# Second expert table's weights split by pairs of neighbouring indices, the first norm applied on turned rows, tiles placed anew (decoder step, one core)

## The chip, the core and the metric

The kernel runs on one core of a Trainium2 chip. TensorE (PE, its weight loads shown as PEld) multiplies, VectorE (DVE), ScalarE (ACT) and GpSimd (POOL) do the elementwise work, SyncE (SP) issues most DMAs, and POOL issues the gathers. The metric is the device time of one execution in microseconds (us); lower is better.

## The reference

One decoder layer for 256 prompt tokens and 32 sample tokens (8 sequences of 4): an input projection feeds 16 RWKV-7 heads and 16 sparse-attention heads, an output projection and a residual norm follow. Then comes the part that the change is about, a mixer over 16384 experts chosen by product keys:

```python
def peer_ffn(x, wq, subkeys, u_tab, v_tab):
    q = (xt @ wq).reshape(n, P_HEADS, 2, P_DKEY // 2)          # 8 heads, two halves of 128
    s = jnp.einsum('nhcd,hckd->nhck', q, subkeys)              # 128 keys for each half
    hv, hix = lax.top_k(s, P_TOPK)                             # 16 of each
    cand = hv[:, :, 0, :, None] + hv[:, :, 1, None, :]
    cand_e = hix[:, :, 0, :, None] * N_KEYS + hix[:, :, 1, None, :]
    tv, tpos = lax.top_k(cand, P_TOPK)                         # 16 experts for each head
    gate = jax.nn.softmax(tv, axis=-1)
    h = gelu(einsum('cd,chkd->chk', xb, u_tab[eb]))            # 128 dots for each token
    return einsum('chk,chkd->cd', gb * h, v_tab[eb])           # 128 weighted rows

x = layer_norm(DEEPNORM_ALPHA * x + h, ln1_g, ln1_b)
f = peer_ffn(x, peer_wq, peer_subkeys, peer_u, peer_v)
x = layer_norm(DEEPNORM_ALPHA * x + f, ln2_g, ln2_b)
```

All data is float32, D_MODEL is 2048. The tables peer_u and peer_v hold 16384 rows of 2048.

## The kernel before

Products are split where accuracy is wanted at a high rate: an operand is cast to float32r (the high part, on ACT), the rest is the operand less that cast (the low part, on DVE or POOL), and three matmuls high-high, high-low, low-high take the place of one in float32. The order on each engine is not the program's: a planner plays the program through on a model of the engines and issues what is ready by priority. `tc.issue_after(x)` puts instructions no earlier than x, `tc.high_priority(offset=n)` lifts them, `keep_in_program_order` pins them. Tiles live in pools that are stacks from the left and from the right of each partition; a tile placed over older ones waits until those are done with. In a pool, the first call for a name sets its place.

The stages from the output projection on, which the change touches:

1. *Output projection* (`out_part`, L1647 to L1676). `out_part(0, BV)` multiplies the RWKV half beside the prompt attention, `out_part(8, YN)` the attention half: 16 pieces of weight, each cast (L1662), split (L1663; every fourth on POOL) and used by 12 matmuls (L1668); sums go into X1 on DVE (L1674, L1676).
2. *Sample chain* (`sample_chain`, L1465 on): the 32 sample tokens go through their own projection, norm, queries and choice (`choose`, `settle`), and then through 32 rounds of two gathers of half rows of peer_u (POOL, `gather`, L454) and two dots on DVE (L1552). It is woven with `out_part(8, YN)`.
3. *First norm of the prompt tokens* (`layer_norm`, L1622): statistics (L1628), root (L1434 to L1438 and L242 to L247), normalising on ACT (L1633), gain and bias on DVE and POOL (L1634, L1635), store to X1D in memory (L1723), turning by PE (L1727), copies to XT (L1731), and casts and splits of six of its 16 blocks to XH, XL (L1639, L1640 in `columns`).
4. *Queries* (from L1745): SKT and QP are placed, X1a is read back from X1D; 16 columns of queries in float32 (L1808, ring `wraw` of four tiles), QP copies (L1809), scores (L1375) into a ring in TB of two heads, and for each head and 128 tokens `choose` on DVE with one large product on POOL (L1410) and `settle` (L1416, L1417). Heads 3 to 8 carry one dot of the gathered part each (L1777).
5. *Dense part of the first table* (`dense`, L1837): for each first key one tile `ur` of nine 128-column blocks (576 KB), three blocks in float32 (L1843), six split (L1850). The other seven blocks of 2048 columns are gathered for each chosen expert (`peer_u_g`, 128 by 896) and dotted on DVE (L1777), 1.5 for each key.
6. *Weighing* (from L1927): 64 groups of four tokens pick their activations out of AW (`pick`, `picked`, `product_of`), apply gelu and gate, and put the weights back (`scaled` on ACT, L1918; `put`, L1924); the first 28 groups carry the rest of the dots, the others the second table's rows of the samples (L1942). Then `norm_quarters` finishes the samples (L1980 to L1991).
7. *Second table* (from L1995): 128 blocks k, each 128 rows by 1408 columns of peer_v (`rows_load`, 704 KB, three buffers), cast (L2034) and split (L2035). For two blocks at once the token weights out of AW, which lies as [128, 2, 256 tokens, 64], are cast (L2031) and split (L2032). 18 matmuls (L2042) take the weights as the stationary operand. The last 640 columns are gathered for each token and expert (`rq`) and added on DVE (L2015). In the middle, x1 and the gain and bias of the last norm are loaded into the part of AW that is done with (L2056, L2060). `fin` adds, norms and stores.

Of the kernel before, what the change touches and what calls it, by code (L numbers as in the profile page):

```python
# [10 lines left out]
F32 = mybir.dt.float32  # L11
# [23 lines left out]
NSO = 4  # L35
PRI = 200
# [114 lines left out]
def hybrid_decode_step(ctx: ExitStack, tc: tile.TileContext, a, outs, dbg=None):  # L151
# [1234 lines left out]
    def choose(t, h, pool, S, TV):  # L1386
# [5 lines left out]
        gp.tensor_copy(HF, HI)  # L1392
        gp.tensor_scalar(HF[:, 0], HF[:, 0], 128.0, None, op0=OP.mult)
# [19 lines left out]
    def settle(t, h, pool, hit):  # L1413

        EF = pool([P, 16], "EF")
        ve.tensor_reduce(EF, hit, AX.X, OP.add)  # L1416
        ve.tensor_scalar(GI[t][:, 16 * h:16 * h + 16], EF, 2.0 if t == 2 else 1.0, None, op0=OP.mult)  # L1417

# [46 lines left out]
    def sample_chain(cx):  # L1465
# [76 lines left out]
        hd = cx([P, 2, 32], "hd")  # L1542
# [5 lines left out]
        for s_ in range(32):  # L1548
# [4 lines left out]
            yield 1  # L1553
        ve.tensor_tensor(hd[:, 0], hd[:, 0], hd[:, 1], OP.add)
# [49 lines left out]
    more_banks(sa=2, pb=1, sao=1, pa=2)  # L1604
    np_ = Pool("np", "left")
# [4 lines left out]
    cx = [Pool("cx", "left")]  # L1610
    lp, oe = Pool("lp", "left"), Pool("oe", "left")
# [10 lines left out]
    def layer_norm(pool, x, g_, b_):  # L1622

        st = pool([P, 4, 6], "lnst", bufs=2)
        mv = pool([P, 2], "lnmv", bufs=2)
        rr = pool([P, 1], "lnrr", bufs=2)
        for q in range(4):
            ve.bn_stats(out=st[:, q, :], in_=x(512 * q, 512))  # L1628
        ve.bn_aggr(out=mv, in_=st.rearrange("p a b -> p (a b)"))
        norm_row(pool, mv, rr)  # L1630
        for q in range(4):
            x_ = x(512 * q, 512)
            sc.activation(x_, x_, AF.Identity, bias=mv[:, 0:1], scale=rr)  # L1633
            ve.tensor_tensor(x_, x_, g_(512 * q, 512), OP.mult)  # L1634
            (gp if q % 2 else ve).tensor_tensor(x_, x_, b_(512 * q, 512), OP.add)  # L1635
# [11 lines left out]
    def out_part(o, src):  # L1647
# [7 lines left out]
        for cq in range(4):  # L1655
# [15 lines left out]
            for t in range(2):  # L1671
# [30 lines left out]
    weave((take(chain, 38), 38), (prompt_attention(), 19), (out_first(), 19))  # L1702
    M_("out")
    fewer_banks(1)
    more_banks(pa=6)
    weave((chain, 32), (out_part(8, YN), 16))
# [4 lines left out]
    XH, XL = (xq([P, NSP, NPR], nm, F32R) for nm in ("XHq", "XLq"))  # L1711
# [7 lines left out]
    for t in range(2):  # L1719
        layer_norm(lp, lambda c0, n: x1c(t, c0, n),  # L1720
                   *(lambda c0, n, nm=nm: gb1[nm, c0 // 1024][:, c0 % 1024:c0 % 1024 + n] for nm in ("ln1_g", "ln1_b")))
        for hf in range(2):
            sy.dma_start(X1D[P * t:P * t + P, 1024 * hf:1024 * hf + 1024], X1[t][hf])  # L1723
        for q in range(4):
            pb = bank("pa")
            for e in range(4):
                pe.transpose(pb[:, 128 * e:128 * e + 128], x1c(t, 512 * q + 128 * e, 128), ident)  # L1727
            tk = slice(P * t, P * t + P)
            p4, e0 = pb.rearrange("p (k t) -> p k t", k=4), max(0, 16 - NDB - 4 * q)
            e1 = min(4, 16 - NDB + NSP - 4 * q)  # L1730
            sc.copy(XT[:, 4 * q:4 * q + 4, tk], p4)  # L1731
            if e1 > e0:
                k4 = slice(4 * q + e0 - 16 + NDB, 4 * q + e1 - 16 + NDB)
                columns(p4[:, e0:e1], XH[:, k4, tk], XL[:, k4, tk])
    oe.close()
    lp.close()
    cx[0].close()
    np_.close()
# [388 lines left out]
```

## Time and profile before

| | |
|---|---|
| three runs | 2503.61, 2513.51, 2522.33 us; median 2513.51 us |
| profiled execution | 2521.09 us; its span 2518.9 us, mean granted PE clock 0.929 |
| busy | PE 2248.0, PEld 1884.6, DVE 1876.1, ACT 962.4, POOL 1374.3 us |
| memory | 683.17 MB moved by DMA, 271 GB/s on average |
| second half of the output projection | 1002.9 to 1061.1 us |
| query products | 1103.4 to about 1238 us |
| dense part | first copy to AW at about 1243 us, last at 1711.8 us |
| second table's matmuls | 1982.1 to about 2496 us |

The page cuts the span into 40 slices of 63 us and gives for each engine the busy share in tenths. A group row gives line, engine, operation, output and input, shape and count, then busy time and the mean ns of one, then the idle time of the engine just before and what ended it. A timeline row gives start, duration, engine, line, operation and, in brackets, the idle time before it and its releaser. A window row gives the busy time of PE, PEld, DVE, ACT and POOL in a stretch, with counts, then the granted PE clock, the DMA share and GB/s. A wait row gives who waited for whom: us in all, times, longest. A line row gives the shortest, median and longest duration in ns, and the first and last start.

### The profile page before, as it was taken

How to read it: one execution, taken by the hardware profiler on the slowest of the kernel's cores; microseconds unless marked ns; L12 is line 12 of the kernel's file. 1: busy time of each engine (PE TensorE's matmuls, PEld its weight loads, DVE VectorE, ACT ScalarE, POOL GpSimd, SP SyncE). 2: the span in 40 equal slices, each digit the busy share in tenths (PEclk: the TensorE clock that was granted, in tenths of full speed). 3: DMA queues.
4: the chain of work that ended last, by engine and by line, in shares of the span. 5: the costliest groups of instructions: out<-in, count | busy, mean ns of one | idle time of the engine just before them, and what ended most of it. 6: DMA issues, size and time to landing. Idle time of an engine off the chain costs nothing.

```text
span 2518.9 us, 44857 instructions
## 1 busy us (share of the span) xinstructions
PE 2248.0 (89%) x16396; PEld 1884.6 (75%) x16396; DVE 1876.1 (74%) x4266; ACT 962.4 (38%) x1847; POOL 1374.3 (55%) x1393
## 2 busy tenths in 40 slices
PE   7988999997888997749999999997689799989996
PEld 7877898874645665538888889996666688868885
DVE  5789756554553356977977777669986699989998
ACT  4433222213332343221133334444566554435453
POOL 5677423242355003754655555555556488868883
PEclk9999999997895897969999999997899899989998
DMA  8777975457468884985489999997678699999995
GB/s 225 223 234 227 270 219 168 118 177 228 168 233 252 282 278 170 344 293 182 134 340 371 370 372 351 357 353 227 205 241 291 219 364 359 361 367 353 359 365 198
DMA packets 327420, 683.17 MB, mean 271 GB/s; under 512 B 82206, under 2 KB 200928, under 8 KB 326400
## 3 DMA queue, kind: packets, MB, share of 16 engines
q1 hardware_dynamic: 246560, 343.63, 41.1%
q0 software_dynamic: 80640, 336.68, 38.2%
q8 instruction: 129, 2.11, 0.3%
q14 instruction: 91, 0.75, 0.1%
HBM read 664.64 MB, written 23.88 MB: 273 GB/s over the span
## 4 chain that ended last, share of the span: by engine, by line
PE 50%; DVE 17%; DMA 9%; POOL 9%; issue 8%; ACT 3%; SPq 1%; POOLq 0%; DVEq 0%; ACTq 0%
PE ph L1850 10%; PE pb L2042 10%; POOL rq L454 6%; PE pj L423 5%; PE ph L1843 3%; PE p L1080 2%; PE pa L1668 2%; DVE rows L1777 2%; PE pa L1924 2%; DVE ul L1640 2%; DMA co<-in_cache_cmp_kv,gidx 2%; PE pj L1808 1%; DVE cw L1552 1%; PE px L1894 1%; PE sa L921 1%
## 5 line engine op out<-in xcount | busy, mean ns | idle before, releaser
L454 POOL DMA_INDIRECT rq<-in_peer_v_g,gi x256 | 404.3, 1579 | 118.0 <-DVE fP L2015 67.8
L454 POOL DMA_INDIRECT rows<-in_peer_u_g,gi x256 | 327.0, 1277 | 249.5 <-DVE rows L1777 206.8
L1777 DVE SCALAR_TENSOR_TENSOR rows<-rows,x1a 128x896 f32<-128x896 f32 x256 | 274.3, 1100 | 2.0 <-DMA rows<-in_peer_u_g,gi 1.9
L423 PE MATMUL pj<-XH,wl 128*128 128x288 f32 (+1 forms) x752 | 231.8, 309 | 13.9 <-DVE wl L418 7.7
L423 PE MATMUL pj<-XH,wh 128*128 128x288 f32 (+1 forms) x752 | 229.7, 306 | 14.0 <-DVE ss L753 6.1
L1850 PE MATMUL ph<-XHd,uh 128*128 128x256 f32 x768 | 236.4, 308 | 0.0
L1850 PE MATMUL ph<-XHd,ul 128*128 128x256 f32 x768 | 224.6, 293 | 8.4 <-DVE ul L1640 3.6
L1640 DVE TENSOR_TENSOR ul<-ur,uh 128x384 fp32r<-128x384 f32 x256 | 133.6, 560 | 128.1 <-ACT uh L1639 88.1
L423 PE MATMUL pj<-XL,wh 128*128 128x288 f32 (+1 forms) x752 | 225.9, 301 | 0.0
L2015 DVE SCALAR_TENSOR_TENSOR fP<-rq,ge,fP 128x640 f32<-128x640 f32 x254 | 223.7, 881 | 2.4
L1850 PE MATMUL ph<-XLd,uh 128*128 128x256 f32 x768 | 217.0, 283 | 0.0
L2042 PE MATMUL pb<-vl,ah 128*128 128x512 f32 (+1 forms) x768 | 206.9, 378 | 0.0
L2042 PE MATMUL pb<-vh,ah 128*128 128x512 f32 (+1 forms) x768 | 187.7, 380 | 20.8 <-ACT vh L2034 20.8
L2042 PE MATMUL pb<-vh,al 128*128 128x512 f32 (+1 forms) x768 | 205.8, 376 | 0.0
L416 ACT CAST wh<-wraw 128x512 fp32r<-128x512 f32 (+1 forms) x188 | 115.0, 616 | 227.0 <-PE pj L423 188.3
L1843 PE MATMUL ph<-Xfd,ur 128*128 128x256 f32 x768 | 187.3, 379 | 2.4 <-DMA ur<-in_peer_u_t 2.4
L2042 PEld LDWEIGHTS pb<-vh,ah 128*128 128x128 f32 x768 | 142.9, 191 | 44.5 <-ACT vh L2034 21.9
L477 DVE SCALAR_TENSOR_TENSOR CA<-co,wbc,CA 128x256 f32<-128x256 f32 x248 | 135.6, 585 | 48.5 <-DMA co<-in_cache_cmp_kv,gidx 48.5
L1850 PEld LDWEIGHTS ph<-XHd,ul 128*128 128x128 f32 x768 | 146.5, 191 | 22.7 <-DVE ul L1640 22.0
L423 PEld LDWEIGHTS pj<-XH,wl 128*128 128x128 f32 (+1 forms) x752 | 143.9, 191 | 25.7 <-DVE wl L418 11.6
L1852 ACT COPY AW<-ph 128x256 f32<-128x256 f32 x128 | 77.8, 608 | 217.4 <-PE ph L1850 204.8
L423 PEld LDWEIGHTS pj<-XH,wh 128*128 128x128 f32 (+1 forms) x752 | 144.2, 192 | 20.7 <-ACT wh L416 6.7
(854 smaller groups left out, 5519.4 us busy)
## 6 DMA issues: line engine op xcount, KB each, us to landing
ur<-in_peer_u_t SPq DMA_DIRECT2D x128, 576.0 KB
wraw<-in_w_in SPq DMA_DIRECT2D x152, 256.0 KB
cw<-in_w_out SPq DMA_DIRECT2D x32, 512.0 KB
wraw<-in_peer_wq SPq DMA_DIRECT2D x32, 512.0 KB
wraw<-in_w_out SPq DMA_DIRECT2D x32, 512.0 KB
cw<-in_peer_wq SPq DMA_DIRECT2D x32, 512.0 KB
wraw<-in_w_in SPq DMA_DIRECT2D x64, 128.0 KB
co<-in_state_win_kv SPq DMA_DIRECT2D x16, 512.0 KB
```

The source lines that it names most:

```text
L416: sc.copy(wh[:, :, :n], w[:, :, :n])
L423: last[2] = pe.matmul(pb[:n, :nt], wi[:, k, :n], xi[(o + k) // 8][:, (o + k) % 8, :nt], start=(o + k == 0 and wi is wh and xi is xh), stop ...
L454: gp.indirect_dma_start(out=dst, out_offset=None, in_=rows_, in_offset=bass.IndirectOffsetOnAxis(ap=ix, axis=0))
L477: ve.scalar_tensor_tensor(d_, x_, w_, d_, op0=OP.mult, op1=OP.add)
L1080: pe.matmul(pb[hs[c], 64 * m:64 * m + 64], lhs(hs[c], m), rhs(hs[c], m), start=True, stop=True)
L1640: return ve.tensor_tensor(xl, pb, xh.bitcast(F32), OP.subtract)
L1777: i_ = ve.scalar_tensor_tensor(r_, r_, 1.0, X1a[t][:, :UG], op0=OP.mult, op1=OP.mult, accum_out=h_)
L1843: pe.matmul(ph[:, :NPR], w[:, e, :], Xfd[:, e - NSP, :], start=(e == NSP), stop=False)
L1850: mm = pe.matmul(ph[:, :NPR], wi[:, e - e0, :], xi[:, e, :], start=False, stop=(e == NSP - 1 and wi is wl))
L1852: return lo_, mm, sc.copy(AW[:, i1 // 64, :, i1 % 64], ph[:, :NPR])
L2015: ve.scalar_tensor_tensor(fP[t], r_, w_, fP[t], op0=OP.mult, op1=OP.add)
L2042: pe.matmul(acc[3 * t + q][:, :n_], wi[:, P * t:P * t + P], xi[:, 512 * q:512 * q + n_], start=(k == 0 and wi is ah and xi is vh), stop=(k ...
```

## The change

- *Second table.* The weights of two blocks are cast and split as [128, tokens, 2] instead of [128, 2, tokens]: AW is read by pairs of words, and TensorE reads its stationary operand at every second word.
- *Late loads of the second table's stage.* Each of the eight loads is placed after the row load of its block.
- *First norm.* Statistics are taken as each column quarter is summed; both roots are taken at once; DVE normalises; PE turns the rows without gain and bias, and ACT applies these while it copies to XT, where they are per-partition numbers. The token rows get gain (DVE) and bias (POOL) afterwards, and POOL stores them to X1D. The casts and splits for the dense part come out of XT, on ACT and POOL, at the end of the queries.
- *Sample dots.* 14 of 32 rounds stay beside the output projection, which is lifted in priority by 400; six are placed after the norm, the others at two for each head in the queries, out of a pool and a copy of the sample rows of their own. The prompt dots there start at head 7, not 3.
- *`choose`, `settle`.* The index casts go to POOL.
- *Weighing.* The last four groups share their scaling between ACT and DVE. The sample norm's loads move to group 46 and into X1a's place.
- *Tiles.* Pools are opened in another order, and names called early, so that tiles lie elsewhere: the first query weights and the first `ur`, `oT`, `v_` and `vh` tiles among them.

The diff, cut to its core:

```diff
@@ choose, settle
-        gp.tensor_copy(HF, HI)
-        gp.tensor_scalar(HF[:, 0], HF[:, 0], 128.0, None, op0=OP.mult)
+        for c in range(2):
+            gp.tensor_scalar(HF[:, c], HI[:, c], k_ if c else k_ * P, 0.0, op0=OP.mult, op1=OP.add)
-        ve.tensor_scalar(GI[t][:, 16 * h:16 * h + 16], EF, 2.0 if t == 2 else 1.0, None, op0=OP.mult)
+        gp.tensor_copy(GI[t][:, 16 * h:16 * h + 16], EF)
@@ sample_chain
-        for s_ in range(32):
+        yield from sample_dots(ring, x4, 0, NSD)                      # NSD = 14
@@ W4
+    lp = Pool("lp", "left")
+    cx = [Pool("cx", "left")]
+    oe = Pool("oe", "left")
     np_ = Pool("np", "left")
-    cx = [Pool("cx", "left")]
-    lp, oe = Pool("lp", "left"), Pool("oe", "left")
@@ out_part
                     ve.tensor_tensor(x_, x_, acc[t], OP.add)
+                    ve.bn_stats(out=lst[:, t, cq, :], in_=x_)
@@ out, ln1
-    weave((chain, 32), (out_part(8, YN), 16))
+    weave((chain, NSD), (out_part(8, YN), 16, 400))
+    wq_ = {(0, o): query_load(0, o) for o in (0, 8)}
     for t in range(2):
-        layer_norm(lp, ...)
-        for hf in range(2):
-            sy.dma_start(X1D[P * t:P * t + P, 1024 * hf:1024 * hf + 1024], X1[t][hf])
+        ve.bn_aggr(out=lmv[:, t, :], in_=lst[:, t].rearrange("p a b -> p (a b)"))
+    ...
+    for t in range(2):
         for q in range(4):
+            normed = ve.tensor_scalar(x_, x_, lrr[:, t:t + 1], lv[:, t:t + 1], op0=OP.mult, op1=OP.add)
             pb = bank("pa")
             for e in range(4):
                 pe.transpose(pb[:, 128 * e:128 * e + 128], x1c(t, 512 * q + 128 * e, 128), ident)
-            sc.copy(XT[:, 4 * q:4 * q + 4, tk], p4)
-            if e1 > e0:
-                columns(p4[:, e0:e1], XH[:, k4, tk], XL[:, k4, tk])
+            for e in range(4):
+                k = 4 * q + e
+                sc.activation(XT[:, k, P * t:P * t + P], pb[:, 128 * e:128 * e + 128], AF.Identity,
+                              bias=prm("ln1_b", 16, k), scale=prm("ln1_g", 16, k))
+    late = sample_dots(lambda: sq_([P, 1024], "sr", bufs=5), sx4, NSD, 32)
+    with tc.issue_after(normed.ins):
+        for _ in take(late, NLD):                                     # NLD = 6
+            pass
+        ...                  # X1 times ln1_g on DVE, plus ln1_b on POOL
+                gp.dma_start(X1D[P * t:P * t + P, 1024 * hf:1024 * hf + 1024], X1[t][hf])
@@ wq
-    TB = up([P, 4, NPR], "TB")
-    X1a = [up([P, UG], f"x1a{t}") for t in range(2)]
-    ...
-    kc, dp, kq = (Pool(nm, "left") for nm in ("kc", "dp", "kq"))
+    up([P, 1024], "rows", bufs=NRW)
+    xa_ = up([P, 2 * UG], "x1a")
+    TB = up([P, 4, NPR], "TB")
+    dp, kc, kq = (Pool(nm, "left") for nm in ("dp", "kc", "kq"))
+    dp([P, NDB, P], "ur", bufs=NUR)
+        if h == 2:
+            for t in range(2):
+                sy.dma_start(X1a[t], X1D[P * t:P * t + P, :UG])
             with tc.issue_after(chosen.ins):
+                for _ in take(late, 2):
+                    pass
-                if h > 2:
+                if h > 6:
                     dot(NDW, 16 * (h - 1), ahead=2)
-    sc.copy(XHd, XH)
-    sc.copy(XLd, XL)
+    for q in range(NSP // 2):
+        k2, x_ = slice(2 * q, 2 * q + 2), XT[:, 16 - NDB + 2 * q:18 - NDB + 2 * q, :]
+        sc.copy(XHd[:, k2, :], x_)
+        gp.tensor_tensor(XLd[:, k2, :], x_, XHd[:, k2, :].bitcast(F32), OP.subtract)
@@ weigh
+            if u < 60 or e % 2:
+                pin(sc.activation(o_, o_, AF.Copy, scale=g_))
+            else:
+                pin(ve.tensor_scalar(o_, o_, g_, None, op0=OP.mult))
+        if s_ == 46:
+            ...              # loads of the sample norm, into xa_ (before: after the loop, into "rows")
@@ V
     vp = Pool("vp", "left")
+    vp([P, FD], "v_", bufs=2)
+    vp([P, FD], "vh", F32R, bufs=2)
-            a2 = [vp([P, 2, NPR], nm, F32R, bufs=2) for nm in ("ah", "al")]
-            aw_ = AW[:, k // 64, :, k % 64:k % 64 + 2].rearrange("p t e -> p e t")
+            a2 = [vp([P, NPR, 2], nm, F32R, bufs=2) for nm in ("ah", "al")]
+            aw_ = AW[:, k // 64, :, k % 64:k % 64 + 2]
-        ah, al = (t_[:, k % 2, :] for t_ in a2)
+        ah, al = (t_[:, :, k % 2] for t_ in a2)
         if k + 3 < P:
-            rows_load(k + 3)
+            ld_ = rows_load(k + 3)
         if 66 <= k < 114 and k % 6 == 0:
+            with tc.issue_after(ld_.ins):
                 ...          # one of the eight late loads
```

More of the change, by code (lines that the diff above doesn't have):

```diff
@@ L1547, in sample_chain, with sample_dots @@
         ve.tensor_scalar(IG, GI[2], 1.0, None, op0=OP.add)
-        for s_ in range(32):
+        yield from sample_dots(ring, x4, 0, NSD)
+    def sample_dots(ring, x4, n0, n1):
+        for s_ in range(n0, n1):
             for q in range(2):
@@ L1609, in hybrid_decode_step @@
         np_(shape, nm, bufs=n_)
-    cx = [Pool("cx", "left")]
-    lp, oe = Pool("lp", "left"), Pool("oe", "left")
     X1 = [[lp([P, 1024], f"x1_{t}{h}") for h in range(2)] for t in range(2)]
+    lst, lmv, lrr, lv = lp([P, 2, 4, 6], "lnst"), lp([P, 2, 2], "lnmv"), lp([P, 2], "lnrr"), lp([P, 2], "lnv")
     def x1c(t, c0, n):
         return X1[t][c0 // 1024][:, c0 % 1024:c0 % 1024 + n]
[L1622 to L1635, printed above, removed]
     def columns(pb, xh, xl):
@@ L1710, in hybrid_decode_step, with query_load @@
     XT = xq([P, 16, NPR], "XT")
[L1711 removed]
+    kw_ = Pool("kw", "right")
+    wring = lambda: kw_([P, 8, P], "wraw", bufs=WB)
+    def query_load(c, o):
+        w = wring()
+        sy.dma_start(w, w_q[:, 128 * c:128 * c + 128].rearrange("(k p) c -> p k c", p=P)[:, o:o + 8])
+        return w
+    wq_ = {(0, o): query_load(0, o) for o in (0, 8)}
     M_("ln1")
@@ L1823, in hybrid_decode_step @@
         settle(t, 7, kc, hit)
+    with tc.issue_after(chosen.ins), tc.issue_after(last_.ins):
+        for _ in late:
+            pass
+        sample_formed()
+    sq_.close()
     kw_.close()
-    sc.copy(XHd, XH)
-    sc.copy(XLd, XL)
+    for q in range(NSP // 2):
+        k2, x_ = slice(2 * q, 2 * q + 2), XT[:, 16 - NDB + 2 * q:18 - NDB + 2 * q, :]
+        sc.copy(XHd[:, k2, :], x_)
+        gp.tensor_tensor(XLd[:, k2, :], x_, XHd[:, k2, :].bitcast(F32), OP.subtract)
     sc.copy(Xfd, XT[:, 16 - NDB + NSP:, :])
@@ L1972, in hybrid_decode_step @@
             smp_add(s_ - 30)
+        if s_ == 46:
+            bs_, gs_, x_ = (xa_[:, 512 * n:512 * n + 512] for n in range(3))
+            for q in range(4):
+                r_, c_ = slice(32 * q, 32 * q + 32), slice(512 * q, 512 * q + 512)
+                sy.dma_start(x_[r_, :], X1D[NPR:NT, c_])
+                for t_, nm in ((gs_, "ln2_g"), (bs_, "ln2_b")):
+                    sy.dma_start(t_[r_, :], bass.AP(tensor=a[nm].tensor, offset=a[nm].offset + 512 * q, ap=[[0, 32], [1, 512]]))
         if s_ == 50:
```

79 lines of the change are left out of this document (42 added, 37 removed).

## The prediction

> **What bounds the kernel now.** I read the page first, then the kernel stretch by stretch. The slices show one hole in PE's row, and the chain by engine says that PE alone carries half of the span.
>
> ```profile
> span 2518.9 us, 44857 instructions
> PE   7988999997888997749999999997689799989996
> PE 50%; DVE 17%; DMA 9%; POOL 9%; issue 8%; ACT 3%; SPq 1%; POOLq 0%; DVEq 0%; ACTq 0%
> ```
>
> The hole (slices of 63 us, the 18th and 19th) lies between the output projection and the query products. PE's timeline and the waits of that stretch (us in all, times, longest) explain it:
>
> ```profile
> 1002.87 0.78 PE L1668 MATMUL pa<-wh,YH 128*128 128x512 f32 x1
> 1060.64 0.39 PE L1668 MATMUL pa<-wh,YL 128*128 128x512 f32 x1
> 1060.87 0.39 PE L1668 MATMUL pa<-wl,YH 128*128 128x512 f32 x1
> PE pa L1727 <- DVE x L1635: 32.6, 4, 13.0
> 1103.43 15.61 PE L1808 MATMUL pj<-XT,wraw 128*128 128x256 f32 x64
> 1131.60 10.04 PE L1808 MATMUL pj<-XT,wraw 128*128 128x256 f32 x32 [12.56 <-ACT QP L1809]
> 1142.36 13.98 PE L1808 MATMUL pj<-XT,wraw 128*128 128x256 f32 x64
> 1156.18 1.05 PE L1375 MATMUL pb<-SKT,QP 128*128 128x128 f32 x8
> 1157.07 13.98 PE L1808 MATMUL pj<-XT,wraw 128*128 128x256 f32 x64
> 1237.51 1.34 PE L1375 MATMUL pb<-SKT,QP 128*128 128x128 f32 x8
> ```
>
> Read it so. The projection ends at 1061; the norm's turnings then wait 33 us for gain and bias on DVE; two query columns run; PE stands another 12.6 us because QP's place is free only after the last sample dot. From 1142 PE runs without a gap: 14.7 us for a head (1142.36 to 1157.07). DVE beside it:
>
> ```profile
> L1552 DVE SCALAR_TENSOR_TENSOR cw<-cw,x 128x1024 f32<-128x1024 f32 x26 | 38.8, 1512 | 1.4 <-DMA cw<-in_peer_u,gi 1.2 <-DMA cw<-in_peer_u,ig 0.2
> L1552 DVE SCALAR_TENSOR_TENSOR cw<-cw,x 128x1024 f32<-128x1024 f32 x32 | 39.8, 1249 | 11.0 <-DMA cw<-in_peer_u,gi 7.7 <-DMA cw<-in_peer_u,ig 3.2
> 1200.00:1220.00 20.00, 20.00 (x102) 17.81 (x101) 19.72 (x85) 2.60 (x7) 12.82 (x19) 1.00 0.62 170
> L1417 DVE TENSOR_SCALAR gi<-EF 128x16 int32<-128x16 f32 x12 | 12.4, 1036 | 0.2
> L1777 DVE SCALAR_TENSOR_TENSOR rows<-rows,x1a 128x896 f32<-128x896 f32 x6 | 10.1, 1680 | 0.0
> ```
>
> The first two rows are the sample dots of 1003 to 1061 and of 1061 to 1131; the others belong to the query heads. There PE is full and DVE is full too (19.72 of 20), so work moved in does not come free.
>
> The last table's stage is paced by PE, with two stalls. In its timeline the matmuls of one row block start every 3.83 us:
>
> ```profile
> 1982.05 2.71 PE L2042 MATMUL pb<-vh,ah 128*128 128x512 f32 x6 [3.66 <-ACT vh L2034]
> 1987.40 0.37 SPq L1950 DMA_DIRECT2D v__20880<-in_peer_v  x1
> 1992.60 1.36 ACT L2034 CAST vh<-v__20880 128x1408 fp32r<-128x1408 f32 x1 [9.56 <-DMA v__20880<-in_peer_v]
> 1999.57 1.44 PE L2042 MATMUL pb<-vh,ah 128*128 128x512 f32 x6
> 2191.08 1.44 PE L2042 MATMUL pb<-vh,ah 128*128 128x512 f32 x6
> 2194.91 1.44 PE L2042 MATMUL pb<-vh,ah 128*128 128x512 f32 x6
> 2224.23 2.64 SPq L2056 DMA_DIRECT2D AW<-x1d  x4
> 2233.65 1.45 PE L2042 MATMUL pb<-vh,ah 128*128 128x512 f32 x6
> 2255.21 1.44 PE L2042 MATMUL pb<-vh,ah 128*128 128x512 f32 x6
> 2242.00:2250.00 8.00, 0.65 (x2) 0.56 (x3) 0.67 (x1) 1.36 (x1) 0.00 (x0) 0.50 1.02 408
> 2300.00:2360.00 60.00, 60.00 (x284) 51.68 (x283) 58.42 (x55) 29.85 (x24) 49.01 (x32) 1.00 0.98 363
> ```
>
> Two blocks should take 7.7 us. At the start they take 17.5 (1982.05 to 1999.57), because rows 1 and 2 are asked for at 1987.40 only. In the middle they take 21.6 (2233.65 to 2255.21): all eight late loads, 4.2 MB, go out together at 2224 and the row loads queue behind them. Otherwise PE has no gap (60.00 of 60) while DVE (58.4) and DMA (0.98) stand just beneath.
>
> **The change, part by part.** Sums are made against the profiled execution, 2521.1 us: the span and 2.2 around it.
>
> *Projection, norm and sample dots.* 192 matmuls at 0.23 (1060.64 to 1060.87) are 44 us, and they took 58. With 14 of the 32 samples in this stretch and the projection raised in priority, I take 47 (bounds 44 and 58): end at 1050, not 1061. The first of the turnings' waits, 13.0 us, runs from there to the first turning; statistics are now taken as columns finish and the gain, the bias and most dots leave it, so I take 6, an estimate between 3 and 13. After them the gain and bias sit in the ACT copies behind the turnings: 32 copies at the 0.32 us of the four in the row below, so 10 us, of which the first query product needs 5 eighths. Start near 1063; 3 us for dots that get between: 1066.
>
> ```profile
> 1969.12 1.28 ACT L1918 ACTIVATE oo<-oo,TB 128x128 f32<-128x128 f32 x4
> ```
>
> Before, the gapless start that would give the same end is 1238.4 less 16 columns at 6.91 and 8 scores at 0.89 (117.7 us), so 1121. The gain here is 55 us. The waits taken away are the 33 and 12.6 above. Gain and bias on the token rows still happen, beside the query products; their stores to X1D go from SP's queue to POOL's. X1a is read back at head 2 on SP, and behind it on that queue stand the later query weights: if a store is late, they are late. The ring of four weight tiles is two columns, 14 us, of cover, so I book nothing.
>
> *What DVE pays.* Heads 1 to 6 take four sample dots each, 4 x 1.25 = 5.0 us; the integer casts leave (12.4 over 8 heads, 1.5), and in four heads a dot (1.7). Heads 3 to 6 carry 1.8 more each on a full DVE. Heads 1 and 2 had no dot to lose, but part of the 9.2 us idle in the row below, and I count 1.8 for them as well: 11 us.
>
> ```profile
> DVE HV L1363 <- ACT TB L1383: 9.2, 3, 5.3
> L1640 DVE TENSOR_TENSOR ul<-ur,uh 128x384 fp32r<-128x384 f32 x256 | 133.6, 560 | 128.1 <-ACT uh L1639 88.1
> ```
>
> Twelve more dots and eight multiplications (20 us) precede the first choice; they fit into the 21 us until the third column ends. Scores rest in a ring of two heads, so lag beyond that reaches PE. Bounds: 0 if the dense stage hides it, where DVE waits 88 us for ACT (second row); 30 if DVE paces everything and only what leaves DVE counts (12.4 + 6.7 of dots + some 6 of norm and splits = 25 of the 55). I take 12, nearer to the count above: gain 43. POOL's queue, with casts, adds and four X1D stores, has gathers behind each; its 12.8 of 20 would cover them.
>
> *Dense start.* XHd, XLd and Xfd come from XT through ACT, idle for most of the query stretch, and POOL; the first table tiles have their place early. I take 0; with the cover gone, three casts and splits at the 616 and 684 ns of the rows under *Pairs* are 4.
>
> *Weighing.* Four dots fewer in the query heads are done here, where DVE is full: the row has 1.09 each, 4.4 lost. The sample norm's loads come some fifteen groups earlier, so the 2.2 us that DVE waited for them goes, and the last four groups split their scaling: two of four 0.32 copies leave ACT, 0.64 x 4 = 2.6. Together 2.2 + 2.6 - 4.4 = +0.4.
>
> ```profile
> L1777 DVE SCALAR_TENSOR_TENSOR rows<-rows,x1a 128x896 f32<-128x896 f32 x49 | 51.4, 1086 | 0.0
> 1963.89 0.69 DVE L1987 SCALAR_TENSOR_TENSOR rows<-rows,fs 128x512 f32<-128x512 f32 x1 [2.20 <-DMA rows<-in_ln_b]
> ```
>
> *Table rows at the start.* Their buffers now lie where the sample rows lay. Those are read for the last time by the products that L1987 (1963.89, above) takes up, so both row blocks can land before 1980. The 9.8 us stall goes; what is late next is POOL's gathers, off PE's path. I take 9, bounds 0 and 10.
>
> *The burst.* One 512 KB load for six blocks: 1.376 + 0.087 MB in 3.83 us asks 382 GB/s; the rows show 363 steadily and 408 in the burst. At 371 it would cost 48 x 0.11 = 5; at 408 nothing. Of 13.9 I take 11, bounds 3 and 14.
>
> *Pairs.* The cast and the split of one table's weights read words 256 bytes apart now:
>
> ```profile
> L2031 ACT CAST ah<-AW x64: 1055/1145/1162, 1979.7 to 2480.5; 128x512 fp32r<-128x512 f32 x64
> L2032 DVE TENSOR_TENSOR al<-AW,ah x64: 1012/1109/1126, 1981.1 to 2481.7; 128x512 fp32r<-128x512 f32 x64
> L416 ACT CAST wh<-wraw 128x512 fp32r<-128x512 f32 (+1 forms) x188 | 115.0, 616 | 227.0 <-PE pj L423 188.3
> L1653 DVE TENSOR_TENSOR YL<-QT,YH 128x512 fp32r<-128x512 f32 x2 | 1.3, 684 | 0.0
> L2042 PEld LDWEIGHTS pb<-vh,ah x768: 187/188/338, 1982.1 to 2493.3; 128*128 128x128 f32 x192
> 1294.29 2.16 PE ph L1850 x18
> ```
>
> At the price of adjacent words they fall from 1145 and 1109 to some 616 and 684 ns, 0.21 us a block off DVE. PE paces, so I book 0; if DVE did, it would be 0.21 x 128 = 27, which PE's row without gaps excludes. PE now loads weights at every second word. A matmul comes every 213 ns (3.83 / 18), and the dense stage gets a load and a matmul into 120 ns (2.16 / 18), so there is room for a load of up to 1.8 times. No row shows a strided load; cost 0 at the one end, and with 376 ns unhidden (188 doubled, as the far-strided cast nearly is) 18 x 0.163 x 128 = +376 us at the other. I take 0, by the room. [...]
>
> Sum: 43 + 0.4 + 9 + 11 = 63; 2521.1 - 63 = 2458. The shown median, 2513.5, is 0.3% under the profiled run: **2450**.
>
> **Rivals.**
> *DVE and POOL pace the heads.* For it: DVE at 19.72 of 20, and instructions stretched beside POOL, L1417's 16 elements to 1036 ns, dots to 1512 and 1680 against 1086. Against: DVE idles 11 us in 1061 to 1131, and dense has room. Only 25 us come, and 5 each from the stalls: 25 + 0.4 + 5 + 5 = 35, 2478. [...]
> *All absorbed.* No lag, both stalls whole: 55 + 0.4 + 10 + 14 = 79, 2434.
> *Slower: strided weight loads.* The price is above: 2450 + 376 = 2826 unhidden. It decides once the pitch passes 240 ns (63 us over 2304 matmuls are 27 ns). At twice dense's 120 it is just there: 2450 + 60 = 2510, no change.
> *It doesn't do it.* Query products still wait for a tile that the late dots or X1D's stores hold. Then only the last stage's 20 remain: 2493.
>
> **Chances.** Forecast 0.42 (own range 2440 to 2462), DVE and POOL 0.20, all absorbed 0.20, loads unhidden 0.06, loads just hidden 0.04, not done 0.08. Faster by over 1% (25 us, about what a measurement of this kernel can tell) are the first three: 0.82; within 1%: 0.12; slower: 0.06. The range, 2415 to 2490, leaves out the loads and most of the undone case.
>
> **What will show it.** Right: query products starting near 1066 without a gap, scores about every 15 us; no PE wait on QP; blocks of 3.83 us from the first, none of 15 near block 66; al near 0.69 us and LDWEIGHTS at 188. Wrong: a pitch above 213, score distances of 17 or more, PE waiting for TB's ring, or gathers that hold POOL up at a full sample ring.

## The result, and the profile after

The changed kernel takes 2497.05 us (median of 17 runs, 2486.80 to 2508.24), the kernel before 2513.84 us in the same session (17 runs, 2501.21 to 2535.25). The ratio is 0.9932 with a 95% interval of 0.9913 to 0.9952: about 17 us, 0.7%, faster. Forecast were 2450 us and a range of 2415 to 2490: the direction is right, the size is not, and the time lies above the range. The profiled execution spans 2496.9 us. Its head, its slices of PE and its chain by engine:

```profile
span 2496.9 us, 44823 instructions
PE   7979999988889997789699999996699799999996
PE 60%; DVE 17%; DMA 8%; issue 7%; ACT 4%; POOL 3%; SPq 1%; DVEq 0%; POOLq 0%; ACTq 0%
```

The slice with a 4 is gone (the 18th has an 8 now), a 6 has come in the 20th (1186 to 1248), and PE carries 60% of the chain instead of 50%. PE's timeline around these slices:

```profile
1049.88 0.39 PE L1668 MATMUL pa<-wl,YH 128*128 128x512 f32 x1
1056.00 5.43 PE L1741 MATMUL pa<-CT,x 128*128 128x128 f32 x32 [5.74 <-DVE x L1738]
1063.27 17.53 PE L1832 MATMUL pj<-XT,wraw 128*128 128x256 f32 x80 [1.83 <-ACT XT L1744]
1100.88 1.22 PE L1378 MATMUL pb<-SKT,QP 128*128 128x128 f32 x4 [4.07 <-ACT QP L1833]
1188.84 1.34 PE L1378 MATMUL pb<-SKT,QP 128*128 128x128 f32 x8
1221.40 0.58 PE L1886 MATMUL ph<-XHd,ul 128*128 128x256 f32 x1 [21.74 <-DVE ul L1640]
```

From the projection's end to the first query product there are 13.4 us now, and the last scores are at 1189 instead of 1238. But behind them is a wait that was not there: PE reaches the dense stage and stands 21.7 us for one split of a table tile on DVE. DVE's timeline, window, group and one row of ACT say why:

```profile
1188.01 0.86 DVE L1366 MAX8 HV<-TB 128x8 f32<-128x128 f32 x4
1199.24 2.78 DVE L1559 SCALAR_TENSOR_TENSOR sr<-sr,sx 128x1024 f32<-128x1024 f32 x1
1201.96 1.22 DVE L1559 SCALAR_TENSOR_TENSOR sr<-sr,sx 128x1024 f32<-128x1024 f32 x1
1205.39 0.86 DVE L1366 MAX8 HV<-TB 128x8 f32<-128x128 f32 x4
...
1100.00:1190.00 90.00, 87.33 (x420) 77.17 (x421) 90.00 (x368) 10.82 (x29) 70.19 (x110) 0.98 0.83 257
...
L1759 DVE TENSOR_TENSOR x<-x,wraw 128x512 f32<-128x512 f32 x8 | 13.2, 1722 | 0.0
...
1097.63 0.65 ACT L1386 COPY TB<-pb 128x256 f32<-128x256 f32 x2 [12.10 <-DMA x1d<-x]
```

One head takes DVE 17.4 us (1188.01 to 1205.39) and PE 14.7; DVE is busy for 90.00 of 90 us. The split that PE waits for stands in DVE's order behind the choices of all eight heads, of which six carry four dots each. Choices also begin late: the first scores are out at 1085 and are copied at 1097.6, when the last store of the token rows has landed, over whose place TB lies.

The last stage, on SP's and PE's timelines, then the weights' rows:

```profile
1954.71 6.01 SPq L2031 DMA_DIRECT2D out<-x1a  x16
1961.09 0.37 SPq L1990 DMA_DIRECT2D v__20899<-in_peer_v  x1
1961.62 0.36 SPq L1990 DMA_DIRECT2D v__20901<-in_peer_v  x1
...
1955.08 2.71 PE L2085 MATMUL pb<-vh,ah 128*128 128x512 f32 x6 [4.22 <-ACT vh L2077]
1972.89 1.44 PE L2085 MATMUL pb<-vh,ah 128*128 128x512 f32 x6
...
2256.74 1.44 PE L2085 MATMUL pb<-vh,ah 128*128 128x512 f32 x6
2262.11 1.56 PE L2085 MATMUL pb<-vh,ah 128*128 128x512 f32 x6 [1.37 <-ACT vh L2077]
2266.44 1.44 PE L2085 MATMUL pb<-vh,ah 128*128 128x512 f32 x6
...
L2075 DVE TENSOR_TENSOR al<-AW,ah x64: 682/692/694, 1954.6 to 2459.3; 128x512 fp32r<-128x512 f32 x64
L2085 PEld LDWEIGHTS pb<-vh,ah x768: 193/193/336, 1955.1 to 2471.4; 128*128 128x128 f32 x192
```

The start is no better: two blocks take 17.8 us, as rows 1 and 2 are asked for at 1961, behind sixteen stores. The one stall of 14 us in the middle has become eight, and each costs 2.0 to 2.7 us (5.37 + 4.33 where two blocks take 7.68). The pairs do what they should: the split is down from 1109 to 692 ns.

**By stage.** Executions differ by tens of us before the change's stages begin, so the stages are laid against the end of the prompt attention (start of its last turning on PE). The kernel before was profiled three times for this; its column is their mean, with the spread. Times in us, worked out from starts in the timelines:

| from, to | forecast gain | before (3 profiles) | changed | gain |
|---|---|---|---|---|
| attention's end to last projection matmul | 11 | 60.6 (58.5 to 62.3) | 63.5 | -2.9 |
| to last scores | 44 | 176.4 (175.7 to 176.7) | 139.0 | 37.4 |
| to last copy to AW (dense) | -12 | 474.5 (474.3 to 475.0) | 493.6 | -19.1 |
| to block 3 of the second table | 9.4 | 294.1 (291.6 to 296.6) | 295.0 | -0.9 |
| block 3 to block 127 | 11 | 488.7 (487.6 to 489.4) | 493.0 | -4.3 |
| to the end | 0 | 26.4 | 26.4 | 0 |
| sum | 63.4 | 1520.7 (1516.6 to 1525.1) | 1510.5 | 10.2 |

So 10 of the 17 us (6 to 15 by the single profiles of before) lie in the stages that the prediction dealt with, and the -0.9 lies inside the spread of before. The other 7 us lie ahead of these stages or in the scatter; see the second and third profiles of before, below.

### The profile page after: what moved, and what is told of

Read it like the earlier page. It is cut to its first block, busy times and chain, and to the rows that moved or that the text cites. A ratio compares the mean times of both kernels' runs of the same rounds, so it can differ in the third digit from the quotient of the medians.

```text
span 2496.9 us, 44823 instructions
## 1 busy us (share of the span) xinstructions
PE 2246.1 (90%) x16396; PEld 1888.6 (76%) x16396; DVE 1851.9 (74%) x4241; ACT 927.4 (37%) x1848; POOL 1373.4 (55%) x1422
## 4 chain that ended last, share of the span: by engine, by line
PE 60%; DVE 17%; DMA 8%; issue 7%; ACT 4%; POOL 3%; SPq 1%; DVEq 0%; POOLq 0%; ACTq 0%
PE pb L2085 17%; PE ph L1886 10%; PE pj L426 8%; PE ph L1879 3%; PE pa L1668 3%; PE p L1083 2%; DVE rows L1803 2%; DMA co<-in_cache_cmp_kv,gidx 2%; DVE sr L1559 2%; PE pa L1963 2%; DVE ul L1640 2%; PE ss L1500 1%; PE px L1930 1%; PE fs L1982 1%; DVE oo L1918 1%
## 5 line engine op out<-in xcount | busy, mean ns | idle before, releaser
L457 POOL DMA_INDIRECT rows<-in_peer_u_g,gi x256 | 332.3, 1298 | 239.5 <-DVE rows L1803 195.2
L457 POOL DMA_INDIRECT rq<-in_peer_v_g,gi x256 | 378.6, 1479 | 141.8 <-DVE fP L2058 80.2
L2085 PEld LDWEIGHTS pb<-vl,ah 128*128 128x128 f32 x768 | 145.2, 195 | 24.5 <-DVE vl L2078 4.5
```

What stands on the lines that cost most here:

```text
L457: gp.indirect_dma_start(out=dst, out_offset=None, in_=rows_, in_offset=bass.IndirectOffsetOnAxis(ap=ix, axis=0))
L2085: pe.matmul(acc[3 * t + q][:, :n_], wi[:, P * t:P * t + P], xi[:, 512 * q:512 * q + n_], start=(k == 0 and wi is ah and xi is vh), stop=(k ...
```

## The experiments

Gains by stage are against the changed kernel's column; ratios are against the kernel before. By the time alone only the late loads in pieces and the two versions with several corrections differ from the changed kernel (0.9913 to 0.9952); the intervals of the others overlap with that one (the burst was run once), and there the stages decide, from one profile of each kernel. Lines left out of the diffs are marked by dots.

**Stores behind the row loads.** A tile `xs` of its own holds the sample block's result, so that its stores can be issued later:

```diff
+    xs = vr([P, 512], "xs")
     ...
     rows_load(1)
     rows_load(2)
+    for q in range(4):
+        for i in range(4):
+            sy.dma_start(outs[1][:, i, 512 * q:512 * q + 512], xs[32 * q + 8 * i:32 * q + 8 * i + 8, :])
```

> The changed kernel, but the sample block's result has a tile of its own beside the table rows' and its 16 stores are issued behind the loads of row blocks 1 and 2. Theory A, SP's queue order: in the changed kernel those two loads go out at 1961.09 and 1961.62 only because they stand behind the 16 stores (1954.71 to 1960.72), which wait for the sample norm; their places have long been free. Then blocks 0 to 2 of the last stage take 8 to 9 us instead of 17.8, and the time falls by 9 to 10 us (0.4%). Theory B, the place or the transfers: the rows' tiles are held by the sample rows of the weighing stage until its end, or the DMAs are too busy there; then the loads go out earlier in the queue and land no earlier, the two blocks still take over 14 us and the time stays within 3 us.

Measured 0.9940 (0.9904 to 0.9976). SP's and PE's timelines of this kernel:

```profile
1915.82 0.35 SPq L1991 DMA_DIRECT2D v__20886<-in_peer_v  x1
1931.18 5.49 SPq L2067 DMA_DIRECT2D out<-xs  x16
1936.79 0.36 SPq L1991 DMA_DIRECT2D v__20928<-in_peer_v  x1
...
1931.55 2.72 PE L2086 MATMUL pb<-vh,ah 128*128 128x512 f32 x6 [4.21 <-ACT vh L2078]
1940.83 1.44 PE L2086 MATMUL pb<-vh,ah 128*128 128x512 f32 x6
1952.11 1.26 PE L2086 MATMUL pb<-vh,ah 128*128 128x512 f32 x5
```

Theory A holds for the cause: with the loads ahead, issued at 1915 instead of behind the stores, the first two blocks take 9.3 us and not 17.8. It misses what is late next: row 3 now stands behind the same sixteen stores, and block 2 lasts 11.3 us. From block 0 to block 3 only 1.9 us are left of the expected 9 to 10 (20.6 against 22.4). From the last copy to AW to block 3 it is 289.8 instead of 295.0, but the other 3.4 us lie ahead of block 0, in a length that runs from 268.5 to 273.6 us over all the profiles.

**Late loads in pieces.** The eight 512-KB loads become 32 of 128 KB, and the multiplications that use them move along:

```diff
-        if 66 <= k < 114 and k % 6 == 0:
+        if k >= 64 and any(64 + 7 * i // 4 == k for i in range(32)):
+            i = next(i for i in range(32) if 64 + 7 * i // 4 == k)
+            n_, p_ = i // 4, i % 4
             with tc.issue_after(ld_.ins):
                 ...
-                c_ = slice(1024 * (n_ % 2), 1024 * (n_ % 2) + 1024)
+                c0 = 1024 * (n_ % 2) + 256 * p_
```

> The changed kernel, but the eight late loads of 512 KB (the token rows and the last norm's gain and bias) go out as 32 pieces of 128 KB, one per 1.75 blocks from block 64 on. Theory A, the size of the piece: each of the eight loads stalls PE for 2.0 to 2.7 us (block distances 5.36 + 4.33 instead of 7.68; 16.7 in all, against 13.9 for the burst before), since three row buffers cover less than one 512-KB transfer at a DMA share of 0.98. In pieces the stage asks (1.376 + 0.075) MB in 3.84 us, 378 GB/s, under the 400 to 408 seen right after a stall: no block over 4.4 us, 12 to 16 us less (0.5 to 0.65%). Theory B, the bytes: the stage moves 361 GB/s and no more, so 4.2 MB cost 11.5 us however they are cut; many blocks grow to about 4.0 us, and the gain is at most 5 us.

Measured 0.9862 (0.9813 to 0.9911). Its window over most of the pieces:

```profile
2230.00:2400.00 170.00, 169.43 (x792) 148.63 (x792) 160.05 (x161) 74.91 (x66) 138.12 (x91) 1.00 1.00 381
```

PE is busy 169.4 of 170 us while 381 GB/s are moved. Blocks 3 to 127 take 477.5 us, 15.5 less; the longest block is 4.58 us (at most 4.4 was expected) instead of 6.00. Theory A holds, and the bytes (theory B) do not set the price: with the big pieces a cycle of six blocks fills the DMAs up to the stall and leaves them at a share of 0.88 behind it, where DVE catches up (8.43 of 8.50 us busy):

```profile
2256.70:2262.20 5.50, 4.13 (x21) 3.34 (x19) 3.77 (x7) 1.92 (x2) 2.65 (x3) 1.00 1.01 405
2262.20:2270.70 8.50, 8.40 (x38) 7.14 (x39) 8.43 (x8) 3.61 (x4) 5.00 (x4) 1.00 0.88 298
```

**The burst again.** The changed kernel without `tc.issue_after(ld_.ins)` around the late loads.

> The changed kernel without the order that ties each late load to its block: the eight late loads of 512 KB are free to go out together, as before. In the last 125 blocks the kernel before takes 488.4 us with the burst and separate weight blocks, the changed kernel 493.0 with spread loads and pairs, and spread loads with separate blocks 504.8. Theory A, the pairs are worth the same either way (11.8 us, by the faster split on DVE): with burst and pairs it takes 475 to 478, so tying the loads to blocks cost 16. Theory B, the pairs help only DVE's catching-up after each of eight stalls: with one stall it takes 486 to 489, and the tying cost 4 to 6.

One run, 2495.48 us. The stall is back in one piece:

```profile
2208.71 1.44 PE L2085 MATMUL pb<-vh,ah 128*128 128x512 f32 x6
2223.39 2.72 PE L2085 MATMUL pb<-vh,ah 128*128 128x512 f32 x6 [10.69 <-ACT vh L2077]
```

Blocks 3 to 127 take 489.1 us, as before the change (488.7). Theory B holds: tying 512-KB loads to blocks cost 3.9 us (4 to 6 were expected), and with the burst the pairs are worth nothing.

**Pairs undone.** The weights as two separate blocks again:

```diff
-            a2 = [vp([P, NPR, 2], nm, F32R, bufs=2) for nm in ("ah", "al")]
-            aw_ = AW[:, k // 64, :, k % 64:k % 64 + 2]
+            a2 = [vp([P, 2, NPR], nm, F32R, bufs=2) for nm in ("ah", "al")]
+            aw_ = AW[:, k // 64, :, k % 64:k % 64 + 2].rearrange("p t e -> p e t")
             ...
-        ah, al = (t_[:, :, k % 2] for t_ in a2)
+        ah, al = (t_[:, k % 2, :] for t_ in a2)
```

> The changed kernel with the weights of the second table laid out as before: two separate blocks of 256 tokens, cast and split by reading words 256 bytes apart, and TensorE reading adjacent words. Theory A, the pairs are worth next to nothing either way: the weight load goes back from 193 to 188 ns, the matmul pitch from 213.3 to 212.6 ns (1.7 us in the stage), the split from 692 to 1109 ns, hidden behind PE except in the catching-up after the late loads (there DVE sets 3.25 us a block, then 3.46); the time stays within 5 us. Theory B, DVE was near enough to PE that the 0.21 us a block matter: up to 27 us slower. Theory C, the loads at every second word are what holds the stage: over 8 us faster.

Measured 0.9981 (0.9949 to 1.0013). Its weight loads and the blocks around one late load:

```profile
L2085 PEld LDWEIGHTS pb<-vh,ah x768: 186/188/338, 1953.9 to 2481.9; 128*128 128x128 f32 x192
...
2230.56 1.45 PE L2085 MATMUL pb<-vh,ah 128*128 128x512 f32 x6
2236.36 1.54 PE L2085 MATMUL pb<-vh,ah 128*128 128x512 f32 x6 [1.80 <-ACT vh L2077]
2242.21 1.44 PE L2085 MATMUL pb<-vh,ah 128*128 128x512 f32 x6
```

The load at adjacent words is 188 ns, at every second word 193; the median block goes from 3.84 to 3.83 us. Theory C falls. Theory A is right where nothing stalls and wrong at the stalls: the two blocks shown take 5.80 + 5.85 (with pairs 5.37 + 4.33), and blocks 3 to 127 take 504.8 us, 11.8 more than with pairs. The pairs pay for DVE's catching-up after the eight stalls that the same change made.

**Without the dots of the heads.** Late dots end with sample 19:

```diff
-    late = sample_dots(lambda: sq_([P, 1024], "sr", bufs=5), sx4, NSD, 32)
+    late = sample_dots(lambda: sq_([P, 1024], "sr", bufs=5), sx4, NSD, NSD + NLD)
+    ve.memset(hd[:, :, NSD + NLD:], 0.0)
```

> The changed kernel without the 24 sample dots (and their 24 gathers) that are issued in the query heads; the hidden values of samples 20 to 31 are set to zero, so part of the sample rows' result is left out. Theory A, DVE paces the heads: with four dots DVE takes 17.4 us a head against PE's 14.7, is full from 1098 to 1221, and the fourth split of the dense stage, which stands behind the heads on DVE, lets PE wait 21.7 us. Without the dots (6.4 us a head) DVE takes about 11 to 12, PE's wait there falls under 4 us, and the dense stage ends 15 to 20 us earlier, as does the kernel. Theory B, the order or POOL: the split waits because of its place in DVE's order behind choices that wait for POOL (index adds, casts) or for the tile of the scores; then a head still takes DVE about 14.7 and more than 10 of the 21.7 us stay.

Measured 0.9880 (0.9823 to 0.9936). PE's waits behind the last scores, and the window of the heads:

```profile
PE ph L1887 <- DVE ul L1640: 2.2, 1, 2.2
...
1090.00:1176.00 86.00, 85.86 (x404) 75.69 (x405) 64.01 (x366) 7.81 (x21) 40.47 (x99) 0.97 0.47 130
```

The wait falls from 21.7 to 2.2 us, DVE has 22 of 86 us free, and from the last scores to the last copy to AW it is 472.8 us, 20.8 less (before: 474.5). Theory A holds: the dots moved into the heads made DVE the slower of the two there. Their 24 gathers went with them; that it was the dots rests on DVE's full row.

**Bias adds on DVE.** Of the norm's gain and bias, the eight adds leave POOL:

```diff
-                        (ve if op_ is OP.mult else gp).tensor_tensor(x_, x_, y_, op_)
+                        ve.tensor_tensor(x_, x_, y_, op_)
```

> The changed kernel with the norm's eight bias adds on DVE instead of POOL. Theory A, POOL stretches DVE and holds the gathers: the eight gain multiplications took 1.72 us each beside POOL's adds, against 0.68 for the same shape alone, and the gathers behind the adds came so late that DVE waited 5.5 us. With all sixteen on DVE at 0.69 (11 us against 13.2) and POOL free, DVE reaches the first choice 4 to 8 us earlier, and PE's wait of 21.7 us for the dense stage's split falls to 14 to 18. Theory B, DVE's own count decides: eight more instructions, 5.5 us, and the wait grows to 25 to 28 us.

Measured 0.9924 (0.9893 to 0.9955). Its group and PE's waits:

```profile
L1759 DVE TENSOR_TENSOR x<-x,wraw 128x512 f32<-128x512 f32 x16 | 10.1, 687 | 0.0
...
PE pj L1832 <- DMA wraw<-in_peer_wq: 10.2, 2, 9.0
PE ph L1886 <- DVE ul L1640: 8.5, 1, 8.5
```

Sixteen operations without POOL's adds beside them take less (10.1 us) than eight with them (13.2). But the mean of 1722 ns in the changed kernel hides what happened there. Its line row and the row of its late dots:

```profile
L1759 DVE TENSOR_TENSOR x<-x,wraw x8: 679/684/8919, 1064.8 to 1077.3; 128x512 f32<-128x512 f32 x8
L1559 DVE SCALAR_TENSOR_TENSOR sr<-sr,sx x36: 1214/1216/2882, 1059.1 to 1204.2; 128x1024 f32<-128x1024 f32 x36
```

Seven of the eight multiplications take 0.68 to 0.73 us, and one takes 8.92, from 1068.50 to 1077.41, while POOL runs six of its adds. All nine profiles with the adds on POOL have such a one, of 8.90 to 8.92 us. The dots behave alike: 2.8 to 2.9 us beside POOL's large product, 2.27 and 2.29 beside its last two adds, 1.21 to 1.23 beside its gathers and casts. So here it was POOL's adds and large products that held DVE's multiplications and dots up, and not its gathers and casts. By what means, no run shows.

Theory B falls. Of A, choices begin 7.0 us earlier after the first query product, and the wait for the split falls further than expected, to 8.5 us. But a query weight now comes 9.0 us late, perhaps since the gathers that POOL no longer holds up are on the DMAs then (not shown); from the first query product to the last copy to AW 3.3 us are left of it (615.9 against 619.2).

**The scores' place.** TB placed ahead of the token rows' tile:

```diff
+    TB = up([P, 4, NPR], "TB")
     xa_ = up([P, 2 * UG], "x1a")
     X1a = [xa_[:, UG * t:UG * t + UG] for t in range(2)]
-    TB = up([P, 4, NPR], "TB")
```

> The changed kernel with the scores' tile TB placed ahead of the token rows' tile instead of behind it. Theory A, the tile: the first scores are out at 1085 but are copied at 1097.6 only, because TB lies where the third and second token blocks lay whose stores (issued on POOL up to 1090.8) have to land first; placed over the block that is stored first, the copy follows the scores at once. DVE's wait of 4.2 us before the first choice and PE's of 4.07 on the query copy go, choices begin 5 to 12 us earlier, and since DVE is full from there to 1221 the wait of 21.7 us in the dense stage shrinks by 4 to 10 us, and so does the time. Theory B, DVE's order: its dots stand ahead of the first choice and wait for gathers held up on POOL, so the choice begins less than 4 us earlier, and the time stays within 3 us.

Measured 0.9929 (0.9887 to 0.9971): by the time not to be told from the changed kernel. In the trace the two waits are gone, and PE's wait for the split is 17.7 us, 4.0 less; from the attention's end to the end of the kernel it is 1507.0 instead of 1510.5. That is A just under its lower end: after the first query product choices begin 4.7 us earlier and not 5 to 12, since the dots ahead of them still wait 5.1 us for gathers. The 3.5 us of the sum lie inside the scatter of such sums.

**Fewer gathers beside the projection.** Samples 6 to 13 reuse gathered rows:

```diff
-                r_, x_, h_ = ring(), x4[:, 1024 * q:1024 * q + 1024], hd[:, q, s_:s_ + 1]
-                gather(r_, uh2, (IG if q else GI[2])[:, s_:s_ + 1])
+                x_, h_ = x4[:, 1024 * q:1024 * q + 1024], hd[:, q, s_:s_ + 1]
+                if not 6 <= s_ < 14:
+                    kept[q] = ring()
+                    gather(kept[q], uh2, (IG if q else GI[2])[:, s_:s_ + 1])
+                r_ = kept[q]
```

> The changed kernel, but eight of the fourteen samples of the projection stretch (samples 6 to 13) take their dots with the rows of sample 5 again: DVE does the same dots, and 16 gathers of 512 KB are left out, so these samples' values are wrong. Theory A, the transfers set the projection's end: from the end of the attention to the end of the projection the changed kernel takes 62.6 us at a DMA share of 0.94 (20.5 MB at 325 GB/s); 8.4 MB less are 24 us at that rate, so PE's own 44 us and its waits for splits become the bound, the stretch takes 47 to 52 us and the kernel is 11 to 15 us shorter than the changed one. Theory B, DVE sets it (splits of the output weights wait behind dots, 10.5 us of PE's waits): DVE has the same work, and the stretch stays at 59 or more.

Measured 0.9923 (0.9877 to 0.9968). The window of the stretch and PE's wait in it:

```profile
985.30:1047.00 61.70, 48.52 (x192) 38.20 (x192) 46.50 (x67) 16.47 (x17) 16.66 (x10) 0.89 0.59 191
...
PE pa L1673 <- DVE wl L1668: 13.2, 4, 9.9
```

The DMA share drops from 0.94 to 0.59 and the stretch still takes 62.5 us. Theory A falls. PE waits for splits of the output weights on DVE, where 21 dots stand between them, as in the changed kernel (10.5 us). B's number holds, but DVE is busy for only 46.5 of the 61.7 us: it is the order on DVE and not its work. In the longest wait, 9.9 us, the split stands behind five dots, and the first of these waited 2.8 us for one of the gathers that are left. The changed kernel has the same on a smaller scale:

```profile
986.43:1050.00 63.57, 52.16 (x195) 39.93 (x195) 47.94 (x67) 16.47 (x17) 40.03 (x26) 0.88 0.94 325
998.25 1.23 DVE L1559 SCALAR_TENSOR_TENSOR cw<-cw,x 128x1024 f32<-128x1024 f32 x1 [2.69 <-DMA cw<-in_peer_u,ig]
999.40 1.22 DVE L1663 TENSOR_TENSOR wl<-wraw,wh 128x1024 fp32r<-128x1024 f32 x1
1000.67 0.79 PE L1668 MATMUL pa<-wl,YH 128*128 128x512 f32 x1 [5.06 <-DVE wl L1663]
```

**The kernel before, twice more.**

> The kernel before, profiled a second time. In its first profile the prompt attention ends at 1003; in the changed kernel and its four variants, whose code up to there is the same, it ends anywhere from 967 to 987. Theory A, scatter from one execution to the next: here it ends well off 1003 too (970 to 995), while the stages behind it keep their lengths within 2 us: 57.7 to the projection's end, 42.6 to the first query product, 134.1 to the last score, 474.3 to the last activation of the dense stage. Theory B, the changed kernel is faster ahead of there, by its new places: it ends within 5 us of 1003 again.

> The kernel before, profiled a third time, for the part ahead of the change. In two profiles its attention ended at 1002 and 983, in eight of the changed kernel and its variants at 967 to 991 (mean 981). Theory A, scatter: it ends between 965 and 1005 and the stages behind it keep their lengths within 2 us each (62.3, 42.0, 133.7, 474.3, and 487.6 for the last 125 row blocks). Theory B, the changed kernel gains ahead of the attention's end: it ends later than 991 again.

The attention ends at 983.5 and 984.9, so both times A. The later stages do keep their lengths from profile to profile, though not all within 2 us: the projection 58.5 to 62.3, up to block 3 291.6 to 296.6. In eleven profiles of the changed kernel and its variants, whose code up to the attention's end is the same, it ends at 963.8 to 990.9, mean 978.7, against a mean of 990.2 in three of before. The scatter of 38 us in all goes with the clock that PE is granted there, as the first profile of before and the kernel with the bias adds on DVE show:

```profile
0.00:1002.30 1002.30, 889.84 (x8669) 709.80 (x8669) 602.54 (x1602) 326.52 (x762) 416.49 (x629) 0.91 0.70 217
0.00:963.80 963.80, 858.71 (x8670) 691.86 (x8670) 607.79 (x1600) 326.22 (x762) 422.78 (x630) 0.94 0.73 225
```

For the same matmuls PE is busy 31 us longer at 0.91 than at 0.94. Over all fourteen profiles the clock up to there runs from 0.906 to 0.937, and the attention's end follows it (correlation -0.94). The three of before have 0.913 in the mean and the eleven others 0.924, which goes with the difference of 11 us. Whether the change has a part in the clock is not shown.

**Corrections together.** First pieces, and the sample block's stores one by one behind the row loads of blocks 6 to 21:

> The changed kernel with both corrections of the last stage: the late loads in 32 pieces of 128 KB, and the sample block's 16 stores spread one by one over blocks 6 to 21, behind the row loads. Theory A, queue order and piece size: with the stores only behind rows 1 and 2 the wait moved to row 3 (11.3 us in place of 3.8, since the stores then stood ahead of that row's load); spread they hold nobody up. From the last dense activation to the start of block 3 280 to 284 us instead of 295, and the 125 blocks behind at 3.84 each, 480 to 484; 27 us less than the changed kernel (1.1%). Theory B, the stage's start is held by the transfers themselves (three row blocks and eight gathers at once, 4.8 MB): the start stays at 289 or more, and the gain is the pieces' 16 us alone.

Measured 0.9817 (0.9775 to 0.9859). To block 3 it is 287.0, 8.0 less but not 280 to 284, and 5.3 of the 8.0 lie between blocks 0 and 3 (17.2 us against 22.4). Neither theory's range has it: the three row buffers are the next limit (row 3 is asked for only when row 0 is cast and split: at 1958.83, with that cast from 1955.65). Blocks 3 to 127 take 482.9, 5.4 more than with the pieces alone, for which no run here shows the reason, and the stages sum to 1492.7, 17.8 less than the changed kernel, where 27 were expected. Then TB's place and the adds on DVE as well:

> The changed kernel with four corrections: late loads in 32 pieces, the sample block's stores spread behind the row loads, TB placed over the block stored first, and the bias adds on DVE. Theory A, they add up: 17.8 us behind the attention for the first two, as measured together, 3.5 for TB, 4 to 8 for the adds; 1485 to 1490 us from the end of the attention instead of 1510.5, and 1518 before. Theory B, TB and the adds remove the same wait of DVE ahead of the first choice: 1489 to 1493.

Measured 0.9855 (0.9802 to 0.9909), 2463.90 us against 2501.36. From the attention's end it is 1486.4 us, inside theory A's range, 24 less than the changed kernel and 34 less than before. B begins at 1489, though, and the sums of the kernel before lie 8.5 us apart, so one profile does not decide between the two. By the time it beats the kernel before and, narrowly, the changed one; it is not told from the version with two corrections, nor from the pieces alone.

## Why the prediction was wrong

Five rows of the table fell short. In two of them the mechanism failed, the late loads and the start of the last stage; in the others the price.

*The burst, +11, came as -4.3.* The step that failed is "one 512 KB load for six blocks ... asks 382 GB/s", which averages over 23 us what arrives at once. A piece of 512 KB meets three row buffers and a DMA share of 0.98; PE stalls, and what the DMAs could then make up is lost in DVE's catching-up. Pieces of 128 KB at nearly the same rate (381 GB/s) cost almost nothing. The rate was right and the grain was missing: this row was off by 15 us, the most of the table.

*Table rows at the start, +9, came as nothing:* blocks 0 to 2 take 22.4 us, and 21.4 to 23.0 before. I looked at when the buffers come free and not at the queue: the change puts no load ahead of the sample block's stores on SP. With that order changed the two blocks took 9.3 us (7.7 without a stall), and the next row was late instead.

*What DVE pays, -12, came as -19.1.* I added 1.8 us a head to a full DVE (there the twelve casts of L1417's row are those of six heads, 2.1 us a head and not 1.5). Six heads with dots are 17.4 to 18.9 us against 14.7, together 19 us over PE, since the first of four dots takes 2.78 us beside POOL's product and not 1.25; and choices began some 13 us after the first scores. The rival "DVE and POOL pace the heads" had the mechanism of this row, and with its other terms (25 + 0.4 + 5 + 5) it asked for 2478. Its 25 us for projection, norm and heads stand against 15.4 measured after the attention's end (-2.9 + 37.4 - 19.1). So its mechanism was the right one here, and even its price was too kind.

*Projection, norm and sample dots, +55, came as 34.5.* The part behind the projection came nearly whole: 37.4 of 44. The query products began 13.4 us after the projection and not 16, and then took some 9 us longer than the sum has it. Of these 6.5 are PE's waits of 4.1 us for QP and 2.4 for query weights between 1063 and 1190. The first is the rival "it doesn't do it" in small: on ACT the copy to QP stands behind the copy to TB, which X1D's stores hold up. The 11 us of the projection did not come. The step that failed is "192 matmuls at 0.23 ... are 44 us": 37 of the 192 come 0.32 to 0.59 us apart, 0.41 in the mean, at a granted clock of 0.88 over the stretch, so the matmuls alone take 48.8 us (45.3 to 48.1 before), more than the 47 that I asked of the whole. PE's stops between them add 14.1 us (12.3 to 13.8 before). I took "14 of the 32 samples" for less than half of the dots, but 14 samples are 28 dots against 26 in the stretch before; 7 of them run ahead of it and 21 are left. Five fewer changed nothing, since raised priority did not move the splits past a dot that waits for its gather. In the two first profiles it even seemed to come (1049.88 for 1060.64), since the attention had ended 16 us earlier in the second one. That was scatter, or at least no gain of this stage; an end time of one profile is no length.

*Pairs, 0, and loads at every second word, 0.* Right where no stall is near. The load takes 193 instead of 188 ns and the block 3.84 instead of 3.83 us, 213 ns a matmul and far from the 240 at which the slower rival begins. The pairs' 11.8 us belong to the stalls.

*Weighing* was forecast at +0.4 and lies with the start in one row of the table, -0.9 together. From the last copy to AW to block 0 it is 272.6 us, and 270.2 to 273.6 before, so a gain of this size can't be seen. What stays open is whether the change has a part in the other 7 of the 17 us, which lie ahead of the attention's end, where the time follows the granted clock.

## What to carry to other kernels

When a stretch runs at a DMA share of 0.98, price a transfer by its size against the buffers that it delays, not by its mean rate, and cut it into pieces before moving it: here 32 of 128 KB for eight of 512 KB brought blocks 3 to 127 from 493.0 to 477.5 us. When a load is to go early, read the issue queue in order: what stands ahead of it there matters as much as the place that it lands in. Here two blocks took 17.8 us with their loads behind sixteen stores and 9.3 with the loads ahead. And before work is put beside a loop whose second engine is full, lay the loop's length on that engine against the bound engine's: 17.4 us and more against 14.7, six times, are 19 of the 21.7 us that PE waited.

## What was not expected of the hardware

- The same code scatters by up to 27 us (963.8 to 990.9) ahead of the end of the attention, with the granted clock (0.937 and 0.918 in these two profiles), while later stages repeat within 1 to 5 us. Lengths of stages from single profiles compared well; end times did not.
- 381 GB/s over 170 us at a DMA share of 1.00, and 405 over the 5.5 us of a stall: at 363 GB/s and 0.98 the DMAs were not yet at their end.
- Eight elementwise products beside POOL's adds took longer on DVE (13.2 us) than products and adds together on DVE (10.1 us), and nearly all of it in one instruction of 8.92 us. Beside POOL's gathers DVE's dots kept their 1.21 us.
- Reading TensorE's weights at every second float32 word cost 5 ns a load here, 193 against 188.
